# Operand sums formed in temporaries, one tile earlier, and three buffers for a pair's second weight tile

## The chip, the cores and the metric

The kernel runs on one core of a Trainium2 chip. The metric is the device time of one execution in microseconds (us). Five queues work side by side: PE (TensorE, matrix products), DVE (VectorE), ACT (ScalarE), POOL (GpSimd) and SP (which issues the weight loads). Each works through its instructions in a fixed order and waits in place for what an instruction needs.

## The reference

Two transformer blocks over 512 tokens of width 1024, all in fp32. The second block has two layers, each a mixer followed by the MLP that the change is in:

```python
for i in range(DEPTH_2):
    hn = _rmsnorm(h, mix_norm_g[i])
    h = h + (_retention(hn, ...) if i % N_MIXERS == 0 else _chunk_attention(hn, ...))
    h = h + _sqrelu_mlp(_rmsnorm(h, mlp_norm_g[i]), mlp_w1[i], mlp_w2[i])

def _sqrelu_mlp(h, w1, w2):      # w1: 1024 x 4096, w2: 4096 x 1024
    u = jax.nn.relu(h @ w1)
    return (u * u) @ w2
```

## The kernel before

**Layout.** Activations lie transposed, 128 channels by 512 tokens to a tile; `xs[0..7]` is the residual stream. An fp32 product is made of three reduced-precision products: each operand has a high half, which ACT copies (line 130), and a low half, which DVE subtracts (line 114). A weight tile `wr` (128x1024) becomes `wh` and `wl`; activations and weight sums become a `pair` of halves.

**An MLP** (`mlp`) goes through four groups. A group makes eight tiles of hidden units from `w1`, then multiplies them with eight tiles of `w2` and adds the results to `xs`. The first six tiles of group 0 are plain products. Every other tile of `w1` is made in pairs by `Quarters.two`: two weight tiles and the two halves of the tokens are treated as a 2x2 matrix of blocks, with seven block products in place of eight, 12 matmuls each. There is one pair in group 0 and four in each of the other groups, 13 in an MLP.

**What a pair needs.** `Quarters.prepare(k)` makes the four sums of the operand's blocks from `xs[k]` and `xs[k+4]`: two scaled copies by ACT (lines 255 and 256), four DVE operations of 128x256, then the split into halves `q0k` and `q1k`. It is called four times in group 0, and its results serve all 13 pairs. `Quarters.weights` loads the pair's first weight tile into `wr` and its second into `b` (tag `qr`), and POOL makes four sums of their blocks, t1, t2, t4, t3 in this order (`total`, line 283), each split into halves by ACT and DVE. Up to here, `prepare` forms its sums in a tile of the same tag `qr`, which has two buffers, and t1 and t2 have two buffers of a tag `qs` of their own; t3 and t4 take temporaries (`tmp`, a pool of eight buffers of 128x512, that everything uses).

**A pair on PE**: product 1 (weights as loaded), copied by ACT into `u`; product 2 (s1, the halves of t1, with sums 0 of all four k), copied into `v`; the pending last product of the pair before; product 3 (s2), added onto product 1 and copied into `u`; a12; s4, after which DVE forms u + z (line 111) and ends tile j; s3, after which DVE forms x1 (line 111, 128x256). The product with a22 is left pending, and then tile j+1 ends. To end a tile is `square_relu`: DVE line 1088, ACT line 1089 (a square), then the halves of `hid[j]`.

**Order.** PE's order is as the program is written. The other queues are ordered by a scheduler that takes priorities and the free buffers into account, so a change of buffers can move instructions on them.

Of the kernel before, what the change touches and what calls it, by code (L numbers as in the profile page):

```python
# [7 lines left out]
F32 = mybir.dt.float32  # L8
# [6 lines left out]
P = 128  # L15
T = 512
# [46 lines left out]
def kernel(  # L63
# [20 lines left out]
    def pair():  # L84
        return ppool.tile([P, 2, T], F32R, tag="p", name="pair")

    def tmp(dt=F32):
        return tpool.tile([P, T], dt, tag="t", name="tmp")

    def bank(n=T):  # L90
        return psum.tile([P, n], F32, tag="b", name="bank")
# [4 lines left out]
    def f32(ap):  # L96
        return ap.bitcast(F32)
# [5 lines left out]
    def g_(name, i):  # L103
        c = GOFF[name] + i
        return gn[:, c:c + 1]
# [4 lines left out]
    def add(out, a, b):  # L110
        dve.tensor_tensor(out=out, in0=a, in1=b, op=ALU.add)  # L111

    def sub(out, a, b):
        return dve.tensor_tensor(out=out, in0=a, in1=b, op=ALU.subtract)  # L114
# [14 lines left out]
    def copy(out, a):  # L129
        act.activation(out, a, AF.Copy)  # L130

    def split(dst, src, rows=slice(0, P), prompt_=False):

        copy(dst[rows, 0, :], src[rows, :])
        last = sub(dst[rows, 1, :], src[rows, :], f32(dst[rows, 0, :]))
        if prompt_:
            prompt.add(last.ins.name)
# [11 lines left out]
    def weight_tiles(pool=None):  # L149
        raw = wpool.tile([P, 8 * P], F32, tag="wr", name="wr")  # L150
        return [raw] + [(pool or wpool).tile([P, 8 * P], F32R, tag=t, name=t) for t in ("wh", "wl")]

    def load_weights(t, src, c):
        raw, hi, lo = t
        sp.dma_start(raw[:, c], src[:, c])
        with tc.high_priority(offset=HW):
            copy(hi[:, c], raw[:, c])
            prompt.add(sub(lo[:, c], raw[:, c], f32(hi[:, c])).ins.name)

    def weights(src, n=8 * P):  # L160
        t = weight_tiles()
        load_weights(t, src, slice(0, n))
        return t[1:]

    def rows(src, mt, k0=0, nk=8):
        return src[mt * P:(mt + 1) * P, k0 * P:(k0 + nk) * P]
# [67 lines left out]
    def together(parts, ends):  # L234

        for i in range(2 * KT - 2):
            next(parts[i % 2])
            yield
        for part, end in zip(parts, ends):
            drain(part)  # L240
            end()
            yield

    class Quarters:
# [6 lines left out]
        def prepare(self, k, gname):  # L251

            hi, lo = (self.pool.tile([P, 4, T // 2], F32R, name=f"q{e}{k}", tag=f"q{e}{k}") for e in range(2))
            p, q = tmp(), tmp()
            act.activation(p, xs[k], AF.Copy, scale=g_(gname, k))
            act.activation(q, xs[k + 4], AF.Copy, scale=g_(gname, k + 4))
            (b11, b12), (b21, b22) = ([a[:, h] for h in HALVES] for a in (p, q))
            t = self.pool.tile([P, 4, T // 2], F32, name="qr", tag="qr", bufs=2)
            sub(t[:, 0, :], b12, b11)
            sub(t[:, 2, :], b22, b12)  # L260
            add(t[:, 1, :], t[:, 2, :], b11)
            sub(t[:, 3, :], b21, t[:, 1, :])
            copy(hi, t)
            sub(lo, t, f32(hi))
            self.sums.append((hi, lo))

        def operand(self, i, j):
# [5 lines left out]
        def weights(self, src, j, k):  # L273

            one = weight_tiles()
            load_weights(one, rows(src, j), slice(0, 8 * P))
            a = one[0]
            b = self.pool.tile([P, 8 * P], F32, name="qr", tag="qr", bufs=2)
            sp.dma_start(b, rows(src, k))
            a11, a12, a21, a22 = a[:, :T], a[:, T:], b[:, :T], b[:, T:]  # L280

            def total(out, x, y, op):
                nc.gpsimd.tensor_tensor(out=out, in0=x, in1=y, op=op)  # L283

            def parts(src):
                pr = pair()
                split(pr, src, prompt_=True)
                return pr[:, 0, :], pr[:, 1, :]

            with tc.high_priority(offset=HQ):  # L290
                t1, t2 = (self.pool.tile([P, T], F32, name="qs", tag="qs", bufs=2) for _ in range(2))
                t3, t4 = tmp(), tmp()
                total(t1, a21, a22, ALU.add)
                s1 = parts(t1)
                total(t2, t1, a11, ALU.subtract)
                s2 = parts(t2)
                total(t4, a12, t2, ALU.subtract)
                s4 = parts(t4)
                total(t3, a11, a21, ALU.subtract)
                s3 = parts(t3)  # L300
                a22 = parts(a22)
            hi, lo = one[1:]
            return (hi[:, :T], lo[:, :T]), (hi[:, T:], lo[:, T:]), a22, s1, s2, s3, s4
# [48 lines left out]
    def pull(gen, n):  # L352
        for _ in range(n):
            next(gen, None)

    def drain(gen):
        for _ in gen:
            pass
# [225 lines left out]
    for kt in range(KT):  # L584
        t = const.tile([P, T], F32, name=f"x{kt}", tag=f"x{kt}")
# [43 lines left out]
    with tc.tile_pool(name="m1", bufs=1) as m1, tc.tile_pool(name="pt1", bufs=1) as ptp:  # L629
# [142 lines left out]
        for i in (1, 0):  # L772
# [3 lines left out]
            for j in range(2):  # L776
                t = tmp()
# [11 lines left out]
        qs = {}  # L789
# [290 lines left out]
    def mlp(i, now, nxt):  # L1080
        norm, hn = now.norm, now.hn
        qpool = tc.tile_pool(name="qp", bufs=1, reuse_waits="tile")
        quarters = Quarters(hn, qpool.__enter__())
        hid = [pair() for _ in range(8)]

        def square_relu(j, ps):
            t = tmp()
            dve.scalar_tensor_tensor(out=t, in0=ps, scalar=0.0, in1=norm.r, op0=ALU.max, op1=ALU.mult)  # L1088
            act.activation(t, t, AF.Square)  # L1089
            split(hid[j], t)  # L1090

        def group(grp):
            r0 = i * 32 + grp * 8
            if grp == 0:

                two = [(bank(), weights(rows(m_w1, r0 + j))) for j in range(2)]
                yield from together([units(ps, w, K8, hn) for ps, w in two],
                                    [lambda j=j, ps=ps: norm.then(lambda: square_relu(j, ps))
                                     for j, (ps, _) in enumerate(two)])
                for j in range(2, 6):  # L1100
                    w = weights(rows(m_w1, r0 + j))
                    ps = bank()
                    yield from units(ps, w, K8, hn)
                    norm.then(lambda j=j, ps=ps: square_relu(j, ps))
                    if j > 2:
                        quarters.prepare(j - 3, now.gname)
                    yield
                quarters.prepare(3, now.gname)
            for j in range(6 if grp == 0 else 0, 8, 2):
                yield from quarters.two(m_w1, r0 + j, r0 + j + 1, lambda u, j=j: square_relu(j, u),  # L1110
                                        lambda u, j=j: square_relu(j + 1, u))

        for grp in range(4):
            gen = group(grp)
            if grp == 0:
                norm.run(gen, *N_MLP[i])
            drain(gen)
            ends = grp == 3 and nxt is None

            def product(mt):  # L1120
                ws, ps = weights(rows(m_w2, i * KT + mt, grp * 8)), bank()
                return units(ps, ws, K8, hid), lambda: second_end(mt, ps)

            def second_end(mt, ps):
                add(xs[mt], xs[mt], ps)
                if ends:
                    final.square(xs[mt])
                elif grp == 3:
                    nxt.take(mt)


            first = together(*zip(*[product(mt) for mt in range(2)]))
            pull(first, 2)
            drain(quarters.last())
            drain(first)
            if grp == 3:
                qpool.__exit__(None, None, None)
            for mt in range(2, KT - 3 if ends else KT):
                w = weights(rows(m_w2, i * KT + mt, grp * 8))
                ps = bank()  # L1140
                drain(units(ps, w, K8, hid))
                add(xs[mt], xs[mt], ps)
                if ends:
                    final.square(xs[mt])
                elif grp == 3:
                    nxt.take(mt)
            if ends:
                finish(hid, [weights(rows(m_w2, i * KT + mt, grp * 8)) for mt in range(KT - 3, KT)])
# [51 lines left out]
    with tc.tile_pool(name="m2", bufs=1, reuse_waits="tile") as m2:  # L1200
        cs = []
        for i in range(2):
            t = m2.tile([P, T], F32, name=f"rc{i}", tag=f"rc{i}")
# [142 lines left out]
    now, nx = nx, Next("mix1")  # L1346
# [224 lines left out]
```

## Time and profile before

| | |
|---|---|
| median of 3 runs | 2018.83 us (2018.65 to 2020.06) |
| profiled execution | 2017.05 us, span 2015.2 us |
| mean granted clock of PE | 0.991 |
| busy | PE 1952.5 us (97%), DVE 1300.4 (65%), ACT 924.6 (46%), POOL 176.2 (9%) |
| MLP of layer 1, of layer 2 | some 1000 to 1350 us, and 1630 to 2015 us |

The span runs from the first to the last instruction. An engine's idle time matters only where PE waits for it.

### The profile page before, as it was taken

The numbers are of one execution on the slowest core, as the hardware profiler recorded it, in microseconds if no ns is written. First come the engines' busy times: TensorE is split into PE (matmuls) and PEld (weight loads), VectorE is DVE, ScalarE is ACT, GpSimd is POOL, SyncE is SP. The second block draws the span as 40 slices with busy tenths as digits, with TensorE's granted clock in tenths as the row PEclk, the third lists the DMA queues.
The fourth block names the chain that finished last, engine by engine and source line by source line (L and its number), as shares of the span: only waits on it lengthen the run. The fifth ranks groups of instructions, "written<-read, shape, count | busy, mean of one in ns | idle before, by whom it ended". The sixth has DMA issues, their size and how long they took to land.

```text
span 2015.2 us, 26327 instructions
## 1 busy us (share of the span) xinstructions
PE 1952.5 (97%) x10284; PEld 1673.0 (83%) x10284; DVE 1300.4 (65%) x2238; ACT 924.6 (46%) x1571; POOL 176.2 (9%) x125
## 2 busy tenths in 40 slices
PE   9999999999999999999997999999999997999998
PEld 7787888888888888888886889898888886889897
DVE  7878953343478565446656667575698976666565
ACT  5776532232245434233444444353576754344352
POOL 1000000000000000000001224220000001324220
PEclk9999999999999999999998999999999998999999
DMA  5122233333232232323222232322322232233321
GB/s 190 58 75 76 84 94 96 104 94 94 91 115 88 85 95 80 102 74 94 74 94 84 94 105 95 108 82 90 98 88 74 71 111 77 94 109 101 105 74 63
DMA packets 59053, 185.46 MB, mean 92 GB/s; under 512 B 6928, under 2 KB 10400, under 8 KB 58928
## 3 DMA queue, kind: packets, MB, share of 16 engines
q1 hardware_dynamic: 53936, 176.02, 27.5%
q10 hardware_dynamic: 4688, 7.40, 1.2%
q8 instruction: 80, 1.31, 0.3%
q14 instruction: 45, 0.37, 0.1%
q0 software_dynamic: 304, 0.36, 0.1%
HBM read 181.56 MB, written 2.20 MB: 91 GB/s over the span
## 4 chain that ended last, share of the span: by engine, by line
issue 57%; PE 30%; DVE 6%; ACT 3%; POOL 2%; DMA 2%; SPq 0%; POOLq 0%; ACTq 0%; DVEq 0%
PE bank L169 7%; PE bank L171 7%; PE bank L170 7%; PE bank L310 6%; DVE wl L114 2%; DMA qr<-in_m_w_dram 1%; DVE pair L114 1%; POOL tmp L283 1%; ACT pair L130 1%; DVE tmp L111 1%; PE bank L526 1%; POOL qs L283 1%; ACT wh L130 1%; DVE tmp L500 0%; DVE tmp L491 0%
## 5 line engine op out<-in xcount | busy, mean ns | idle before, releaser
L169 PE MATMUL bank<-pair,wh 128*128 128x512 f32 (+1 forms) x2134 | 816.4, 383 | 0.2 <-ACT pair L130 0.2
L171 PE MATMUL bank<-pair,wh 128*128 128x512 f32 (+1 forms) x2134 | 807.6, 378 | 0.5 <-DVE pair L114 0.3
L170 PE MATMUL bank<-pair,wl 128*128 128x512 f32 (+1 forms) x2134 | 806.4, 378 | 0.0
L130 ACT ACTIVATE wh<-wr 128x1024 fp32r<-128x1024 f32 (+5 forms) x329 | 324.1, 989 | 653.2 <-PE bank L171 407.7
L114 DVE TENSOR_TENSOR wl<-wr,wh 128x1024 fp32r<-128x1024 f32 (+5 forms) x329 | 383.4, 1168 | 157.1 <-ACT wh L130 155.9
L171 PEld LDWEIGHTS bank<-pair,wh 128*128 128x128 f32 x2134 | 401.4, 188 | 77.0 <-DVE pair L114 1.7
L169 PEld LDWEIGHTS bank<-pair,wh 128*128 128x128 f32 x2134 | 401.9, 188 | 70.9 <-ACT pair L130 0.8
L170 PEld LDWEIGHTS bank<-pair,wl 128*128 128x128 f32 x2134 | 402.0, 188 | 70.4 <-DVE wl L114 0.5
L114 DVE TENSOR_TENSOR pair<-tmp,pair 128x512 fp32r<-128x512 f32 (+1 forms) x208 | 171.2, 830 | 63.7 <-ACT pair L130 60.7
L130 ACT ACTIVATE pair<-tmp 128x512 fp32r<-128x512 f32 (+1 forms) x240 | 149.8, 628 | 130.7 <-POOL tmp L283 54.8
L310 PE MATMUL bank<-q,pair 128*128 128x256 f32 x1248 | 166.4, 287 | 38.8 <-ACT pair L130 26.6
L310 PEld LDWEIGHTS bank<-q,pair 128*128 128x128 f32 x1248 | 157.0, 192 | 44.2 <-ACT pair L130 27.1
L111 DVE TENSOR_TENSOR x<-x,bank 128x512 f32<-128x512 f32 (+1 forms) x99 | 66.0, 669 | 170.0 <-PE bank L171 170.0
L283 POOL TENSOR_TENSOR qs<-qr 128x512 f32<-128x512 f32 x26 | 40.9, 1573 | 1478.0 <-DMA qr<-in_m_w_dram 1478.0
L108 DVE TENSOR_TENSOR tmp<-bank,rb 128x512 f32<-128x512 f32 (+1 forms) x76 | 50.2, 666 | 103.9 <-PE bank L171 101.3
L310 PE MATMUL bank<-pair,wh 128*128 128x256 f32 x416 | 83.0, 283 | 0.0
L169 PE MATMUL bank<-wh,pair 128*128 128x512 f32 x200 | 79.3, 396 | 0.6 <-ACT tmp L130 0.6
L171 PE MATMUL bank<-wl,pair 128*128 128x512 f32 x200 | 78.0, 390 | 0.0
L170 PE MATMUL bank<-wh,pair 128*128 128x512 f32 x200 | 77.9, 390 | 0.0
L494 ACT ACTIVATE tmp<-tmp,small 128x512 f32<-128x512 f32 (+1 forms) x96 | 53.4, 556 | 34.1 <-DVE small L491 32.9
L310 PEld LDWEIGHTS bank<-pair,wh 128*128 128x128 f32 x416 | 67.8, 190 | 0.8 <-ACT tmp L130 0.2
L1089 ACT ACTIVATE tmp<-tmp 128x512 f32<-128x512 f32 x64 | 40.1, 627 | 61.1 <-DVE tmp L1088 61.1
(182 smaller groups left out, 2010.2 us busy)
## 6 DMA issues: line engine op xcount, KB each, us to landing
wr<-in_m_w_dram SPq DMA_DIRECT2D x102, 512.0 KB, 3.7
wr<-in_r_qkg_dram SPq DMA_DIRECT2D x32, 512.0 KB, 3.5
qr<-in_m_w_dram SPq DMA_DIRECT2D x26, 512.0 KB, 3.7
wr<-in_w_gate_dram SPq DMA_DIRECT2D x20, 512.0 KB, 3.5
wr<-in_w_up_dram SPq DMA_DIRECT2D x20, 512.0 KB, 3.5
wr<-in_w_down_dram SPq DMA_DIRECT2D x16, 512.0 KB, 3.4
wr<-in_r_v_dram SPq DMA_DIRECT2D x16, 512.0 KB, 3.5
wr<-in_r_out_dram SPq DMA_DIRECT2D x16, 512.0 KB, 3.7
```

What stands on the lines that cost most here:

```text
L108: dve.tensor_tensor(out=out, in0=a, in1=b, op=ALU.mult)
L111: dve.tensor_tensor(out=out, in0=a, in1=b, op=ALU.add)
L114: return dve.tensor_tensor(out=out, in0=a, in1=b, op=ALU.subtract)
L130: act.activation(out, a, AF.Copy)
L169: pe.matmul(out, lhsT=ah, rhs=bh, start=start, stop=False)
L170: pe.matmul(out, lhsT=al, rhs=bh, start=False, stop=False)
L171: pe.matmul(out, lhsT=ah, rhs=bl, start=False, stop=stop)
L283: nc.gpsimd.tensor_tensor(out=out, in0=x, in1=y, op=op)
L310: pe.matmul(out, lhsT=x[:, c], rhs=y, start=start and k + i == 0, stop=k == 3 and i == 2, skip_group_check=True)
L494: act.activation(s[:, :n], s[:, :n], AF.Exp, bias=self.mx[:, col], scale=-1.0, accum_out=self.sm[:, col])
L526: pe.matmul(o, lhsT=a, rhs=b, start=j == 0 and a is v, stop=j == NT - 1 and a is v)
L1089: act.activation(t, t, AF.Square)
```

## The change

`prepare` forms its four sums in two temporaries `s` and `t` of 128x512, with two sums each, and splits each of them on its own; it is called for k = 0 to 3 after the plain tiles 2 to 5, where before it came for k = 0 to 2 after tiles 3 to 5 and for k = 3 behind them. `b` alone uses the tag `qr` now, with three buffers. t1 and t2 become temporaries as well, and the tag `qs` is gone.

```diff
--- before.py
+++ after.py
@@ -255,13 +255,14 @@
             act.activation(p, xs[k], AF.Copy, scale=g_(gname, k))
             act.activation(q, xs[k + 4], AF.Copy, scale=g_(gname, k + 4))
             (b11, b12), (b21, b22) = ([a[:, h] for h in HALVES] for a in (p, q))
-            t = self.pool.tile([P, 4, T // 2], F32, name="qr", tag="qr", bufs=2)
-            sub(t[:, 0, :], b12, b11)
-            sub(t[:, 2, :], b22, b12)
-            add(t[:, 1, :], t[:, 2, :], b11)
-            sub(t[:, 3, :], b21, t[:, 1, :])
-            copy(hi, t)
-            sub(lo, t, f32(hi))
+            s, t = (tmp().rearrange("p (e t) -> p e t", e=2) for _ in range(2))
+            sub(s[:, 0, :], b12, b11)
+            sub(t[:, 0, :], b22, b12)
+            add(s[:, 1, :], t[:, 0, :], b11)
+            sub(t[:, 1, :], b21, s[:, 1, :])
+            for e, a in ((slice(0, 2), s), (slice(2, 4), t)):
+                copy(hi[:, e, :], a)
+                sub(lo[:, e, :], a, f32(hi[:, e, :]))
             self.sums.append((hi, lo))
 
         def operand(self, i, j):
@@ -275,7 +276,7 @@
             one = weight_tiles()
             load_weights(one, rows(src, j), slice(0, 8 * P))
             a = one[0]
-            b = self.pool.tile([P, 8 * P], F32, name="qr", tag="qr", bufs=2)
+            b = self.pool.tile([P, 8 * P], F32, name="qr", tag="qr", bufs=3)
             sp.dma_start(b, rows(src, k))
             a11, a12, a21, a22 = a[:, :T], a[:, T:], b[:, :T], b[:, T:]
 
@@ -288,8 +289,7 @@
                 return pr[:, 0, :], pr[:, 1, :]
 
             with tc.high_priority(offset=HQ):
-                t1, t2 = (self.pool.tile([P, T], F32, name="qs", tag="qs", bufs=2) for _ in range(2))
-                t3, t4 = tmp(), tmp()
+                t1, t2, t3, t4 = (tmp() for _ in range(4))
                 total(t1, a21, a22, ALU.add)
                 s1 = parts(t1)
                 total(t2, t1, a11, ALU.subtract)
@@ -1102,10 +1102,8 @@
                     ps = bank()
                     yield from units(ps, w, K8, hn)
                     norm.then(lambda j=j, ps=ps: square_relu(j, ps))
-                    if j > 2:
-                        quarters.prepare(j - 3, now.gname)
+                    quarters.prepare(j - 2, now.gname)
                     yield
-                quarters.prepare(3, now.gname)
             for j in range(6 if grp == 0 else 0, 8, 2):
                 yield from quarters.two(m_w1, r0 + j, r0 + j + 1, lambda u, j=j: square_relu(j, u),
                                         lambda u, j=j: square_relu(j + 1, u))
```

**DVE between the first and the second pair of group 1.** The rows are of the first MLP, before. `tmp_9389` and `bank_9387` belong to the pair that ends, `pair_9494`, `_9498` and `_9501` are the low halves of s4, s3 and a22 of the pair that begins, `pair_9620` and `pair_9624` those of s1 and s2 of the third pair, `pair_8664` and `pair_8665` are hidden tiles.

```order
L111 TENSOR_TENSOR tmp_9389<-tmp_9389,bank_9388 128x512
L111 TENSOR_TENSOR bank_9387<-tmp_9390,bank_9387 128x256
L1088 SCALAR_TENSOR_TENSOR tmp_9455<-tmp_9389,rb_8768 128x512
L114 TENSOR_TENSOR pair_9494<-tmp_9484,pair_9494 128x512
L114 TENSOR_TENSOR pair_9498<-tmp_9483,pair_9498 128x512
L114 TENSOR_TENSOR pair_9501<-qr_9479,pair_9501 128x512
L114 TENSOR_TENSOR pair_9620<-qs_9615,pair_9620 128x512
L114 TENSOR_TENSOR pair_8664<-tmp_9455,pair_8664 128x512
L1088 SCALAR_TENSOR_TENSOR tmp_9546<-bank_9387,rb_8768 128x512
L114 TENSOR_TENSOR pair_9624<-qs_9616,pair_9624 128x512
L114 TENSOR_TENSOR pair_8665<-tmp_9546,pair_8665 128x512
```

The same place after the change; `pair_9498` and `pair_9502` are s1 and s2 of the pair that begins, `pair_9506`, `_9510` and `_9513` its s4, s3 and a22:

```order
L111 TENSOR_TENSOR tmp_9401<-tmp_9401,bank_9400 128x512
L111 TENSOR_TENSOR bank_9399<-tmp_9402,bank_9399 128x256
L1088 SCALAR_TENSOR_TENSOR tmp_9467<-tmp_9401,rb_8768 128x512
L114 TENSOR_TENSOR pair_9498<-tmp_9493,pair_9498 128x512
L114 TENSOR_TENSOR pair_9502<-tmp_9494,pair_9502 128x512
L114 TENSOR_TENSOR pair_9506<-tmp_9496,pair_9506 128x512
L114 TENSOR_TENSOR pair_9510<-tmp_9495,pair_9510 128x512
L114 TENSOR_TENSOR pair_9513<-qr_9491,pair_9513 128x512
L114 TENSOR_TENSOR pair_8664<-tmp_9467,pair_8664 128x512
L1088 SCALAR_TENSOR_TENSOR tmp_9558<-bank_9399,rb_8768 128x512
L114 TENSOR_TENSOR pair_8665<-tmp_9558,pair_8665 128x512
```

The low halves of s1 and s2 stood a pair ahead of their use, and now stand behind the end of the pair before (the `bank_9399` row, line 111) and ahead of everything else of their own pair.

**POOL, the sums of the second to fourth pair of group 1.** Before (a `DVE` in the brackets is a wait for a DVE instruction, a `DMAHW` one for a load, and `qs_9615`, `qs_9616` are t1 and t2 of the third pair):

```order
L283 TENSOR_TENSOR qs_9615<-qr_9613 128x512 [waits DMAHW4_49,DVE_49,Pool_49]
L283 TENSOR_TENSOR tmp_9484<-wr_9473,qs_9482 128x512
L283 TENSOR_TENSOR tmp_9483<-wr_9473,qr_9479 128x512
L283 TENSOR_TENSOR qs_9616<-qs_9615,wr_9607 128x512 [waits DMAHW5_49,DVE_49,Pool_49]
L283 TENSOR_TENSOR qs_9749<-qr_9747 128x512 [waits DMAHW0_49,DVE_49,Pool_49]
L283 TENSOR_TENSOR tmp_9618<-wr_9607,qs_9616 128x512
L283 TENSOR_TENSOR tmp_9617<-wr_9607,qr_9613 128x512
```

After the change, t1, t2, t4, t3 of the third pair and the first two of the fourth:

```order
L284 TENSOR_TENSOR tmp_9627<-qr_9625 128x512 [waits DMAHW7_49,DVE_49,Pool_49]
L284 TENSOR_TENSOR tmp_9628<-tmp_9627,wr_9619 128x512 [waits DMAHW6_49,DVE_49,Pool_49]
L284 TENSOR_TENSOR tmp_9630<-wr_9619,tmp_9628 128x512 [waits DVE_49,Pool_49]
L284 TENSOR_TENSOR tmp_9629<-wr_9619,qr_9625 128x512 [waits DMAHW5_49,DVE_49]
L284 TENSOR_TENSOR tmp_9761<-qr_9759 128x512 [waits DMAHW5_49,DVE_49,Pool_49]
L284 TENSOR_TENSOR tmp_9762<-tmp_9761,wr_9753 128x512 [waits DMAHW7_49,DVE_49,Pool_49]
```

Every sum waits for DVE now, since every one takes a temporary that some earlier low half must have been read from; before, in groups 1 to 3, only t1 and t2 did so, for the `qs` buffer of the pair before.

**DVE ahead of the first pair**, before: `q12` and `q13` are low halves of the sums for k = 2 and 3, `pair_8979` that of s1.

```order
L111 TENSOR_TENSOR qr_8959<-qr_8959,tmp_8955 128x256
L114 TENSOR_TENSOR wl_9092<-wr_9090,wh_9091 128x1024
L114 TENSOR_TENSOR q12_8941<-qr_8946,q02_8940 128x1024
L114 TENSOR_TENSOR qr_8959<-tmp_8956,qr_8959 128x256
L114 TENSOR_TENSOR q13_8954<-qr_8959,q03_8953 128x1024
L114 TENSOR_TENSOR pair_8979<-qs_8974,pair_8979 128x512
L114 TENSOR_TENSOR pair_8983<-qs_8975,pair_8983 128x512
L114 TENSOR_TENSOR pair_8987<-tmp_8977,pair_8987 128x512
```

And after the change (`tmp_8968` and `tmp_8969` are `s` and `t` of k = 3, `pair_8991` is the low half of s1, `pair_8995` that of s2):

```order
L111 TENSOR_TENSOR tmp_8968<-tmp_8969,tmp_8964 128x256
L114 TENSOR_TENSOR pair_8669<-tmp_8957,pair_8669 128x512
L114 TENSOR_TENSOR pair_8991<-tmp_8986,pair_8991 128x512
L114 TENSOR_TENSOR tmp_8969<-tmp_8965,tmp_8968 128x256
L114 TENSOR_TENSOR pair_8995<-tmp_8987,pair_8995 128x512
L114 TENSOR_TENSOR pair_8999<-tmp_8989,pair_8999 128x512
L114 TENSOR_TENSOR pair_9003<-tmp_8988,pair_9003 128x512
L114 TENSOR_TENSOR pair_9006<-qr_8984,pair_9006 128x512
L114 TENSOR_TENSOR q13_8963<-tmp_8968,q03_8962 128x512
L114 TENSOR_TENSOR q13_8963<-tmp_8969,q03_8962 128x512
```

The halves of the last operand sums, which stood ahead of the weights' halves, stand behind all of them.

**SP, the weight loads between retention and the first MLP**, one piece of the difference; `qr` is the load of `b`:

```order
 L155 DMA wr<-in_r_qkg_dram 128x1024 x4
-L155 DMA wr<-in_r_out_dram 128x1024 x8
-L155 DMA wr<-in_m_w_dram 128x1024 x11
-L279 DMA qr<-in_m_w_dram 128x1024 x2
+L155 DMA wr<-in_r_out_dram 128x1024 x2
+L280 DMA qr<-in_m_w_dram 128x1024 x3
+L155 DMA wr<-in_r_out_dram 128x1024 x6
+L155 DMA wr<-in_m_w_dram 128x1024 x12
```

The first three loads of `b` move ahead of the MLP's own loads, in among those of retention's output weights. The second MLP has the same move into the loads of `a_out`.

## Rows read from the trace of the kernel before

**Rows 1.** The page, part 1: busy us, share, instructions.
```profile
PE 1952.5 (97%) x10284; PEld 1673.0 (83%) x10284; DVE 1300.4 (65%) x2238; ACT 924.6 (46%) x1571; POOL 176.2 (9%) x125
```

**Rows 2.** Waits of PE over the span: waited for, us in total, times, longest.
```profile
PE bank L310 <- ACT pair L130: 26.6, 2, 13.5
PE bank L310 <- ACT tmp L130: 10.3, 12, 1.7
```

**Rows 3.** Timeline, first pair of the first MLP: start, us, engine, line, operation.
```profile
1073.26 0.69 DVE L1088 SCALAR_TENSOR_TENSOR tmp<-bank,rb 128x512 f32<-128x512 f32 x1 [0.19 <-PE bank L171]
...
1079.94 1.22 DVE L114 TENSOR_TENSOR q<-qr,q 128x1024 fp32r<-128x1024 f32 x1
...
1081.23 3.01 SPq L279 DMA_DIRECT2D qr<-in_m_w_dram  x2
...
1082.62 1.23 DVE L114 TENSOR_TENSOR q<-qr,q 128x1024 fp32r<-128x1024 f32 x1 [1.12 <-ACT q L130]
1085.82 1.25 POOL L283 TENSOR_TENSOR qs<-qr 128x512 f32<-128x512 f32 x1 [1045.66 <-DMA qr<-in_m_w_dram]
1087.11 0.63 ACT L130 ACTIVATE pair<-qs 128x512 fp32r<-128x512 f32 x1 [4.52 <-POOL qs L283]
...
1087.79 0.58 PE L310 MATMUL bank<-q,pair 128*128 128x256 f32 x1 [13.14 <-ACT pair L130]
...
1089.02 1.22 PE L310 MATMUL bank<-q,pair 128*128 128x256 f32 x4 [0.65 <-DVE pair L114]
```

**Rows 4.** Windows around that restart; before DMA share and GB/s stands PEclk.
```profile
1080.00:1086.00 6.00, 0.00 (x0) 0.00 (x0) 2.72 (x4) 1.06 (x1) 0.18 (x1) 0.50 0.63 203
...
1092.00:1094.00 2.00, 2.00 (x16) 1.85 (x16) 1.85 (x3) 1.64 (x4) 1.50 (x1) 0.98 0.47 119
```

**Rows 5.** PE's timeline, group 1: the first products of two successive pairs.
```profile
1151.33 0.28 PE L310 MATMUL bank<-pair,wh 128*128 128x256 f32 x1
...
1161.68 0.28 PE L310 MATMUL bank<-pair,wh 128*128 128x256 f32 x1
```

**Rows 6.** DVE's timeline in the pairs of group 1.
```profile
1162.09 0.67 DVE L111 TENSOR_TENSOR tmp<-tmp,bank 128x512 f32<-128x512 f32 x1
1162.69 0.42 DVE L111 TENSOR_TENSOR bank<-tmp,bank 128x256 f32<-128x256 f32 x1
...
1163.80 2.38 DVE L114 TENSOR_TENSOR pair<-tmp,pair 128x512 fp32r<-128x512 f32 x2
1166.11 0.68 DVE L114 TENSOR_TENSOR pair<-qr,pair 128x512 fp32r<-128x512 f32 x1
...
1182.11 1.22 DVE L114 TENSOR_TENSOR wl<-wr,wh 128x1024 fp32r<-128x1024 f32 x1 [0.26 <-ACT wh L130]
```

**Rows 7.** POOL's timeline in the same stretch.
```profile
1161.05 2.28 POOL L283 TENSOR_TENSOR tmp<-wr,qr 128x512 f32<-128x512 f32 x1
1163.29 1.75 POOL L283 TENSOR_TENSOR qs<-qs,wr 128x512 f32<-128x512 f32 x1
```

**Rows 8.** ACT's timeline in the same stretch.
```profile
1168.63 0.63 ACT L1089 ACTIVATE tmp<-tmp 128x512 f32<-128x512 f32 x1 [1.49 <-DVE tmp L1088]
1169.17 0.36 ACT L130 ACTIVATE tmp<-bank 128x256 f32<-128x256 f32 x1
...
1169.95 1.05 ACT L130 ACTIVATE wh<-wr 128x1024 fp32r<-128x1024 f32 x1
```

**Rows 9.** Groups of DVE by shape, 1190 to 1225: busy, mean ns, idle before.
```profile
L114 DVE TENSOR_TENSOR pair<-tmp,pair 128x512 fp32r<-128x512 f32 x2 | 3.1, 1552 | 0.3 <-ACT pair L130 0.2
```

**Rows 10.** Windows ahead of the second MLP; last DMA share and GB/s.
```profile
1622.00:1631.00 9.00, 9.00 (x41) 7.46 (x40) 7.34 (x13) 5.23 (x9) 0.00 (x0) 1.00 0.19 66
1631.00:1634.00 3.00, 3.00 (x15) 2.46 (x15) 2.90 (x6) 2.58 (x5) 0.00 (x0) 1.00 0.57 175
```

**Rows 11.** Timeline at the second MLP's second weight tile.
```profile
1638.77 1.23 DVE L114 TENSOR_TENSOR wl<-wr,wh 128x1024 fp32r<-128x1024 f32 x1
...
1640.33 0.39 PE L170 MATMUL bank<-pair,wl 128*128 128x512 f32 x1
```

## The prediction

> **What bounds the kernel now.** I read the page's busy times first: PE is busy for 97% of the span and no other engine for more than 65% [rows 1], so a change counts only where it lengthens or shortens a wait of PE. The list of PE's waits comes next. Two lines of it belong to the pairs (line 310): one long wait ahead of the first pair of each MLP, 26.6 us in two, and 10.3 us in twelve short waits for an ACT copy into a temporary, two in each of the six groups 1 to 3 [rows 2]. These 36.9 us are what the change can touch.
>
> The timeline of the first pair tells what the long wait is for. PE has run dry 13.14 us before 1087.79. The low halves for k = 2 are DVE's 1079.94 row; they are the last reader of a `qr` buffer, so SP issues the load of `b` at 1081.23, POOL starts t1 at 1085.82, ACT's copy is at 1087.11, PE gets one matmul at 1087.79 and the rest from 1089.02 [rows 3]. Behind this chain a second one is hidden: the low halves for k = 3, which the same product needs, are made from 1082.62 for 1.23 us [rows 3]. So without the late load the product could have ended its wait only at 1083.9 even then. The windows show PE's granted clock at 0.50, the 1.2 GHz level, in 1080 to 1086, after some microseconds without a matmul, and at 0.98 in 1092 to 1094 [rows 4]. So what resumes before 1092 may run at half rate.
>
> For the steady pairs, one product 1 stands at 1151.33 and the next at 1161.68: 10.35 us for seven products where PE hardly waits, 1.48 each [rows 5].
>
> **A. The first pair: -5.5 us in both MLPs together.** The load of `b` leaves the path: it has buffers of its own and is issued long before. What is late next is DVE, by its new order. The plain tile 5 ends where it did, and DVE's line 1088 for it starts at 1073.26 [rows 3]. Behind it stand, start to start: itself 0.6, a `wl` 1.14 (the row of 1.22 [rows 6], less the overlap of some 0.08 between rows that follow each other at once), three operations of 128x256 at 0.42 (the nearest row of this size [rows 6]), a hidden tile's low half 0.6 (0.68 alone [rows 6]); that is 1076.85. Then s1's low half, one more operation of 0.42, the low halves of s2, s4, s3 and a22, and only then k = 3. POOL works on the sums meanwhile (1.25 us alone, 1.75 to 2.28 beside DVE [rows 3, 7]), so I cost these five as contended, 1.45 each (below): 1076.85 + 5 x 1.45 + 0.42 + 0.6 = 1085.1 for the first half of k = 3, which product 2 needs. Before, the three matmuls that need k = 3 came some 1.8 us after 1089.02, eight matmuls later at half rate (0.21 from the row of four [rows 3]), at 1090.8. Gain 5.7 us. From it goes the clock: if PE stays at half rate until 1092 as before, 6.9 us of work are worth 3.45, where before 1.2 us were worth 0.6, a loss of 2.85. Net 2.8 for each MLP, 5.5 for two. Ends: 0, if PE's scattered matmuls come later still or the clock stays low for longer; -15, if the clock never falls and the five low halves run half alone.
>
> **B. The steady pairs: +27 us.** Formerly a pair's s1 and s2 were made up to a pair ahead, from buffers that nobody else used. Now POOL's t1 can start only when an earlier low half has been read, so each POOL sum is released by a DVE subtraction of the running pair, and POOL's four sums run under the four subtractions that follow. At the same time s1 and s2 of the beginning pair stand in DVE's queue behind x1, which needs the last product of the pair before. I walk one cycle of DVE and ACT from the start of one s1 low half to the next; a DVE row of 0.68 counts 0.61, start to start.
>
> s1 0.61. s2 must wait for its high half, which ACT copies behind the square of tile j (0.63 [rows 8], a copy about as much): s2 starts at 1.33 and ends its turn at 1.94. Then s4, s3, a22 and hidden tile j, all under POOL. Price of one: 0.61 if alone; 1.15 by the two that took 2.38 us beside POOL's 1163.29 row, which covers only their first part [rows 6, 7]; 1.55 in the w2 tiles, where POOL ran throughout [rows 9]. I take 1.36, between the last two, since POOL's four sums at 1.75 are longer than the four subtractions: 1.94 + 5.44 = 7.38. Line 1088 for tile k is behind them, 8.06. ACT squares it (0.63) and only then copies product 3 into `u` (0.36 [rows 8]): 9.0. PE's s3 product overwrites what this copy reads, and PE would be ready at 7.9 (six products of 1.48 after product 1, which starts 1.0 ahead of s1: x1 at 0.34 and line 1088 at 0.61). Stall 1.1. ACT goes on with k's high half and the `wh` of 1.05 [rows 8] until 10.5; DVE's `wl` (1.22 [rows 6]) to 11.7; u + z 0.60 and x1 0.34 (0.67 and 0.42 [rows 6]), line 1088 0.61: the next s1 starts at 13.25, and is ready at 13.9 where PE, after its stall, has wanted it since 11.9. Stall 1.9. A cycle is 13.25 against 10.35: 2.9 us more. A group has two such cycles, and a first s1 that is 0.35 late: 2 x 2.9 + 0.35 = 6.15. Six groups: 36.9. The 10.3 us of short waits go [rows 2], since they are of the same kind and are contained in the walk: +26.6, say +27.
>
> Ends: with 0.61 each the cycle is 10.25, nothing but the 0.35 stays, 2.1 - 10.3 = -8. With 1.55 each it is 14.0, 7.65 a group, 45.9 - 10.3 = +36.
>
> A rule speaks to this price. The Trainium skill (page "SBUF — State Buffer", section "Who interferes with whom") says that DVE with two SBUF inputs and GpSimd share a port pair as an exclusive lock. If that meant a whole POOL sum ahead of each subtraction, the row of 1.55 [rows 9] would have been 0.68 + 1.25 = 1.93, so the trace shows less than strict turns; that case is the third rival.
>
> **C. The loads: +1 us.** Three loads of `b` (128x1024 fp32, 0.52 MB each) move in among those of `a_out`, ahead of the second MLP. In 1622 to 1631 66 GB/s flowed, and 175 just behind [rows 10]: room for 109 GB/s x 9 us = 0.98 MB of their 1.57; the rest holds the MLP's first weights up by 0.59 MB / 175 GB/s = 3.4 us if none of it went earlier. The second tile's `wl` ends at 1640.00 and PE uses it at 1640.33 [rows 11], so 0.3 us are free. Ends 0 and 3 for each MLP; I take 1 for both, because earlier stretches have room too. Splitting `prepare`'s halves in two pieces adds eight ACT and eight DVE rows in an MLP's one-time preparation; they are in walk A.
>
> **Sum.** 2017.05 - 5.5 + 27 + 1 = 2039.5 for the profiled execution. The runs' median is 1.78 above that execution, so 2041.3 in terms of the median: 2041.
>
> **Rivals.** (1) Contention half as wide: POOL covers two of the four subtractions. The cycle is 11.75, 1.4 over; 6 x (2.8 + 0.35) - 10.3 = +9, and the time 2023. For it: POOL's sums wait for loads before, and any such shift would move them. Against: their waits are now for DVE itself.
> (2) Other side, faster: POOL's sums fall into DVE's free time (DVE is idle for 35% of the span [rows 1]), the cycle stays under 10.35, B is -8, and the first pair gains in full with the clock up, 2 x 6.2: 2018.83 - 8 - 12.4 = 1998. It decides at the price of 0.63 for a subtraction in the cycle, where the cycle is 10.35. Against: every row of a subtraction beside POOL is well above.
> (3) Strict turns: 1.93 per subtraction, cycle 15.5, 5.2 over; 6 x (10.4 + 0.35) - 10.3 = +54, and the time 2068.
> (4) The change does not do what it says for the first pair: PE waits for k = 3 as long as it waited for the load, A is 0: 2047. For it: k = 3 now stands last on DVE.
>
> **How the numbers follow.** Chances: forecast 0.63, rival (1) 0.12, (2) 0.10, (3) 0.07, (4) 0.08. The likeliest case's own range is 2030 to 2050 (B's price of 1.2 to 1.55, A's ends in part). The range reaches down to (1) and up past (4), 2018 to 2056; it leaves out (2), (3) and some of each tail. A change of under 0.2%, 4 us, is about what a measurement of this kernel can't tell from none: half of (1) and some tail of (2) lie there, 0.08. Faster is (2) for the rest and a little of B's low tail, 0.11. Slower is 0.81.
>
> **What would show it.** In the changed profile: PE's one long wait ahead of a first pair is replaced by two or three of 3 to 4 us, the last of them for a DVE low half of `q`, and the next products end some 3 us earlier than before relative to tile 5. In groups 1 to 3 PE waits for a DVE `pair` (line 114) about 1.9 us and for an ACT `tmp` about 1.1 us in two pairs of each group. POOL's rows (line 284) lie under DVE rows of 1.2 to 1.6 us. PE's clock stays at 1.00 in these pairs. The prediction is wrong if DVE's subtractions between s2 and line 1088 take under 1 us each, if POOL's sums come ahead of the running pair, or if PE's short stalls pull the clock to 0.5, which would add to the time beyond the range.

## The result and the profile after

| | before | changed |
|---|---|---|
| median | 2018.91 us (4 runs) | 2039.65 us (2038.91 to 2040.86, 4 runs) |
| ratio | | 1.0102, 95% interval 1.0085 to 1.012 |
| profiled execution, span | 2017.05, 2015.2 us | 2039.02, 2037.0 us |
| mean granted clock | 0.991 | 0.992 |

The change makes the kernel 20.7 us slower. The forecast was 2041 us, with 0.81 for slower.

Where the time went can be read from PE's timelines: the stretch from the start of the first to the start of the last matmul of the pairs (line 310), for the lone pair of group 0 and for the four pairs of each other group. The two MLPs are set one after the other.

| us | before | changed | difference |
|---|---|---|---|
| first pair | 27.35, 27.73 | 23.97, 24.05 | -7.1 |
| groups 1 to 3 | 43.65, 44.44, 43.40, 44.21, 44.44, 43.29 | 48.75, 48.73, 48.74, 48.74, 48.73, 48.73 | +29.0 |
| span | 2015.2 | 2037.0 | +21.8 |

The two differences make 21.9, so what happened elsewhere comes to little in all. PE's list of waits says the same (waited for, us in total, times, longest), where before it had [rows 2]:

```profile
PE bank L310 <- DVE pair L114: 27.0, 20, 3.2
PE bank L310 <- ACT tmp L130: 12.7, 12, 1.1
PE bank L310 <- ACT pair L130: 7.1, 2, 3.9
...
PE bank L310 <- DVE q L114: 3.8, 2, 1.9
```

The two waits of 13 us are gone, and 20 waits for DVE's low halves have come, with twelve for ACT's copies, as many as before and longer on the mean (12.7 us in all for 10.3), though the longest is shorter.

**A steady pair.** PE's timeline of the changed kernel, two successive pairs of group 1 (start, us, operation, and in brackets the idle time before it and its releaser):

```profile
1150.07 4.63 PE L310 MATMUL bank<-q,pair 128*128 128x256 f32 x35 [0.17 <-DVE pair L114]
...
1158.61 1.69 PE L310 MATMUL bank<-q,pair 128*128 128x256 f32 x12 [1.04 <-ACT tmp L130]
...
1163.47 4.62 PE L310 MATMUL bank<-q,pair 128*128 128x256 f32 x35 [1.63 <-DVE pair L114]
```

From one product 2 to the next it is 13.40 us, where before two successive pairs stood 10.35 us apart if no wait fell between them [rows 5]. There are two stalls in it, one of 1.04 for ACT's copy into `u` ahead of s3, and one of 1.63 for the low half of s1. DVE's timeline over the same pair:

```profile
1148.39 0.43 DVE L111 TENSOR_TENSOR bank<-tmp,bank 128x256 f32<-128x256 f32 x1
1148.72 0.69 DVE L1088 SCALAR_TENSOR_TENSOR tmp<-tmp,rb 128x512 f32<-128x512 f32 x1
1149.33 0.69 DVE L114 TENSOR_TENSOR pair<-tmp,pair 128x512 fp32r<-128x512 f32 x1
1150.63 3.00 DVE L114 TENSOR_TENSOR pair<-tmp,pair 128x512 fp32r<-128x512 f32 x3 [0.62 <-ACT pair L130]
1153.55 1.77 DVE L114 TENSOR_TENSOR pair<-qr,pair 128x512 fp32r<-128x512 f32 x1
1155.25 1.78 DVE L114 TENSOR_TENSOR pair<-tmp,pair 128x512 fp32r<-128x512 f32 x1
1156.95 0.68 DVE L1088 SCALAR_TENSOR_TENSOR tmp<-bank,rb 128x512 f32<-128x512 f32 x1
...
1162.13 0.68 DVE L1088 SCALAR_TENSOR_TENSOR tmp<-tmp,rb 128x512 f32<-128x512 f32 x1
...
1180.97 0.68 DVE L114 TENSOR_TENSOR pair<-tmp,pair 128x512 fp32r<-128x512 f32 x1
```

Here the queue can be read as the order has it: x1 (1148.39, 128x256) must wait for the pair before, line 1088 for tile j follows, then s1 (1149.33), a wait of 0.62 for ACT, s2, s4, s3 (three in 3.00 us), a22 1.77, the hidden tile j 1.78, and only at 1156.95 line 1088 for tile k, on which ACT's copy into `u` waits. From 1148.72 to 1162.13 it is 13.41 us, DVE's cycle. The last row is the same subtraction two cycles on, when POOL's sum had ended at 1180.50: it takes 0.68 us, where the one at 1155.25 takes 1.78. POOL's timeline:

```profile
1151.45 1.62 POOL L284 TENSOR_TENSOR tmp<-qr 128x512 f32<-128x512 f32 x1 [20.39 <-DVE pair L114]
1153.15 1.62 POOL L284 TENSOR_TENSOR tmp<-tmp,wr 128x512 f32<-128x512 f32 x1
1154.85 1.63 POOL L284 TENSOR_TENSOR tmp<-wr,tmp 128x512 f32<-128x512 f32 x1
1157.10 1.28 POOL L284 TENSOR_TENSOR tmp<-wr,qr 128x512 f32<-128x512 f32 x1 [0.62 <-DVE pair L114]
```

The first and the fourth sum begin as one of DVE's subtractions gives up a temporary; the second and third follow the sum before them at once. The first three run from 1151.45 to 1156.48, just while DVE is at s3, a22 and j. A window over such a pair has the clock in the third column from the end: it stays up through these stalls.

```profile
1149.00:1163.00 14.00, 11.63 (x92) 10.87 (x90) 11.64 (x14) 6.82 (x14) 6.14 (x4) 1.00 0.15 46
```

**The first pair.** PE's timeline has three waits in place of the long one [rows 3]:

```profile
1078.00 0.56 PE L310 MATMUL bank<-q,pair 128*128 128x256 f32 x1 [3.11 <-ACT pair L130]
1081.79 2.50 PE L310 MATMUL bank<-q,pair 128*128 128x256 f32 x10 [3.23 <-DVE pair L114]
1086.21 3.14 PE L310 MATMUL bank<-q,pair 128*128 128x256 f32 x13 [1.92 <-DVE q L114]
...
1091.71 1.59 PE L310 MATMUL bank<-pair 128*128 128x256 f32 x12
```

DVE's timeline, with the low halves for k = 2, line 1088 of tile 5, the hidden tile and s1, the low halves of s2, s4, s3, then a22, and last the two of k = 3:

```profile
1072.64 2.39 DVE L114 TENSOR_TENSOR q<-tmp,q 128x512 fp32r<-128x512 f32 x2
1074.95 0.68 DVE L1088 SCALAR_TENSOR_TENSOR tmp<-bank,rb 128x512 f32<-128x512 f32 x1
...
1079.37 2.37 DVE L114 TENSOR_TENSOR pair<-tmp,pair 128x512 fp32r<-128x512 f32 x2
...
1081.99 1.88 DVE L114 TENSOR_TENSOR pair<-tmp,pair 128x512 fp32r<-128x512 f32 x3
1083.80 1.75 DVE L114 TENSOR_TENSOR pair<-qr,pair 128x512 fp32r<-128x512 f32 x1
1085.47 1.28 DVE L114 TENSOR_TENSOR q<-tmp,q 128x512 fp32r<-128x512 f32 x2
```

PE goes on at 1086.21 with the last matmul of product 2, after the first of the two low halves for k = 3, as the order had it. It is the only one of the twelve that needs this half: one and ten have run by then, and the row of 13 is that one and the twelve of product 3. The windows show the clock at the 1.2 GHz level from 1078 on, and up again between 1090 and 1092:

```profile
1078.00:1080.00 2.00, 0.56 (x1) 0.26 (x1) 1.97 (x5) 0.52 (x1) 0.78 (x2) 0.51 0.71 219
...
1090.00:1092.00 2.00, 2.00 (x12) 2.00 (x12) 0.00 (x0) 0.09 (x1) 0.00 (x0) 0.57 0.00 0
```

### The profile page after: what moved, and what is told of

Same layout as the page of the kernel before. It is cut to its first block, busy times and chain, and to the rows that moved or that the text cites. A ratio compares the mean times of both kernels' runs of the same rounds, so it can differ in the third digit from the quotient of the medians.

```text
span 2037.0 us, 26315 instructions
## 1 busy us (share of the span) xinstructions
PE 1962.6 (96%) x10284; PEld 1677.1 (82%) x10284; DVE 1325.7 (65%) x2246; ACT 920.9 (45%) x1579; POOL 181.3 (9%) x125
## 4 chain that ended last, share of the span: by engine, by line
PE 74%; DVE 14%; ACT 6%; issue 5%; POOL 0%; DMA 0%; POOLq 0%; ACTq 0%; DVEq 0%
PE bank L169 22%; PE bank L171 22%; PE bank L170 22%; PE bank L310 5%; DVE pair L114 4%; DVE wl L114 3%; ACT pair L130 2%; ACT wh L130 1%; DVE tmp L111 1%; DVE tmp L1088 1%; PE bank L526 1%; ACT tmp L494 1%; PE bank L507 1%; DVE pt L114 1%; DVE tmp L491 1%
## 5 line engine op out<-in xcount | busy, mean ns | idle before, releaser
L114 DVE TENSOR_TENSOR pair<-tmp,pair 128x512 fp32r<-128x512 f32 (+1 forms) x260 | 220.3, 862 | 71.9 <-ACT pair L130 70.2
L310 PE MATMUL bank<-q,pair 128*128 128x256 f32 x1248 | 174.1, 291 | 50.6 <-DVE pair L114 27.0
L130 ACT ACTIVATE pair<-tmp 128x512 fp32r<-128x512 f32 (+1 forms) x292 | 177.8, 624 | 96.2 <-DVE tmp L1306 26.0
L284 POOL TENSOR_TENSOR tmp<-qr 128x512 f32<-128x512 f32 x26 | 43.2, 1662 | 1538.5 <-DVE tmp L114 1032.8
L111 DVE TENSOR_TENSOR tmp<-tmp 128x512 f32<-128x512 f32 (+1 forms) x98 | 60.4, 617 | 14.7 <-ACT tmp L379 13.8
```

What stands on the lines that cost most here:

```text
L310: pe.matmul(out, lhsT=x[:, c], rhs=y, start=start and k + i == 0, stop=k == 3 and i == 2, skip_group_check=True)
```

## The experiments

Each was run beside the kernel before on the same chip, whose medians were 2018.6, 2017.6 and 2018.5 us in the three sets; ratios are to these. A statement's line number can differ by one between the kernels: 309 or 311 stands for 310, and 1089 for 1088.

**e1: the change without its last part.** t1 and t2 keep `qs`, and `b` has two buffers, for which the room suffices.

```diff
-            b = self.pool.tile([P, 8 * P], F32, name="qr", tag="qr", bufs=3)
+            b = self.pool.tile([P, 8 * P], F32, name="qr", tag="qr", bufs=2)
...
-                t1, t2, t3, t4 = (tmp() for _ in range(4))
+                t1, t2 = (self.pool.tile([P, T], F32, name="qs", tag="qs", bufs=2) for _ in range(2))
+                t3, t4 = tmp(), tmp()
```

Expected: 

> The change without its last part: prepare's sums in temporaries and one tile earlier, b with two buffers of its own, but t1 and t2 keep the two buffers of qs. My theory (the loss is that t1 and t2 took temporaries): the steady pairs are as before, with PE's short waits back at some 10 us in twelve and no DVE waits of 1.6 us; the first pair keeps its gain of 3 us or more in each MLP. 2012 us (2008 to 2016). Rival (the loss comes from prepare's temporaries, or from the loads that moved): the time stays at 2035 or above.

Measured 2007.64 us (2006.28 to 2008.79), ratio 0.9947 (0.993 to 0.9963). Faster than the kernel before, and just under the range expected. PE's waits:

```profile
PE bank L311 <- ACT tmp L130: 9.9, 12, 1.7
PE bank L311 <- ACT pair L130: 7.0, 2, 3.9
...
PE bank L311 <- DVE q L114: 3.9, 2, 1.9
PE bank L311 <- DVE pair L114: 2.3, 2, 1.2
```

The short waits are back where they were [rows 2] and the six groups take 262.95 us in all, against 263.43 before. The two first pairs take 21.43 and 21.61 us, 12.0 less than before, and 5.0 less than in the changed kernel. What has shrunk is the wait for the low half of s1, 1.2 us at most where it was 3.2. POOL's t1 and t2 run as soon as the loads are there, far ahead of the first pair, and only the sums in temporaries are left for the end of tile 5:

```profile
983.20 1.29 POOL L284 TENSOR_TENSOR qs<-qr 128x512 f32<-128x512 f32 x1 [941.39 <-DMA qr<-in_m_w_dram]
1058.85 1.30 POOL L284 TENSOR_TENSOR qs<-qs,wr 128x512 f32<-128x512 f32 x1 [74.36 <-DMA wr<-in_m_w_dram]
1075.10 1.59 POOL L284 TENSOR_TENSOR tmp<-wr,qs 128x512 f32<-128x512 f32 x1 [14.95 <-DVE tmp L114]
```

So the loss isn't in prepare's temporaries nor in the loads. (The first pair begins 2.4 us later in this execution than before, and 1.6 us later in e2, whose work up to there is that of the kernel before. Some 1.5 us of either arise between 168 and 174 us, where the mean granted clock is 0.72 in both and 1.00 before; in e1 the rest is there by 30 us. Both lie far ahead of what the edits touch.)

**e2: the last part alone**, in the kernel before:

```diff
-                t1, t2 = (self.pool.tile([P, T], F32, name="qs", tag="qs", bufs=2) for _ in range(2))
-                t3, t4 = tmp(), tmp()
+                t1, t2, t3, t4 = (tmp() for _ in range(4))
```

Expected: 

> The last part alone: the kernel before with t1 and t2 in temporaries. My theory: the cycles of 13.4 us in the steady pairs are there in full, the long wait of 13 us ahead of each first pair stays, 2018.9 + 27 = 2046 us (2040 to 2050). Rival: the pairs are slow only together with the other parts, 2019 us.

Measured 2048.74 us (2047.52 to 2050.44), ratio 1.015 (1.0135 to 1.0165), 30.2 us slower. The waits of both kinds stand side by side, the long one of the first pair and the many of the steady pairs:

```profile
PE bank L309 <- ACT pair L130: 26.9, 2, 13.5
PE bank L309 <- DVE pair L114: 21.8, 20, 1.6
PE bank L309 <- ACT tmp L130: 12.6, 12, 1.1
```

The six groups take 292.35 us, as in the changed kernel (292.42). With e1 this splits the change: temporaries for t1 and t2 cost some 29 us, and the rest of the change is a gain.

**e3: the sums on DVE.** In the changed kernel:

```diff
-                nc.gpsimd.tensor_tensor(out=out, in0=x, in1=y, op=op)
+                dve.tensor_tensor(out=out, in0=x, in1=y, op=op)
```

Expected: 

> The changed kernel with the four sums of a pair's weights made by DVE in place of POOL, so that POOL never runs beside DVE, and DVE has four operations of 0.6 us more in each pair. My theory (DVE's subtractions take 1.7 in place of 0.6 us while POOL runs, some 3.3 us a pair): that falls away and 2.4 us come in, so a cycle goes from 13.4 to 12.6 us, and the time to about 2030 us (2024 to 2036). Rival (contention costs nothing, the order of the queue does): a cycle is 2.4 us longer, 15.8, and the time 2065 or more.

Measured 2023.4 us (2021.8 to 2025.45), ratio 1.0025 (1.0015 to 1.0036), just under the range expected and 16 us less than the changed kernel, although DVE has 104 operations more. DVE's timeline, one cycle from line 1088 to line 1088:

```profile
1148.45 0.69 DVE L1088 SCALAR_TENSOR_TENSOR tmp<-tmp,rb 128x512 f32<-128x512 f32 x1
...
1150.43 0.69 DVE L114 TENSOR_TENSOR pair<-tmp,pair 128x512 fp32r<-128x512 f32 x1
...
1152.85 1.89 DVE L114 TENSOR_TENSOR pair<-tmp,pair 128x512 fp32r<-128x512 f32 x3
1154.65 0.68 DVE L114 TENSOR_TENSOR pair<-qr,pair 128x512 fp32r<-128x512 f32 x1
1155.26 0.68 DVE L1088 SCALAR_TENSOR_TENSOR tmp<-bank,rb 128x512 f32<-128x512 f32 x1
...
1160.32 0.69 DVE L1088 SCALAR_TENSOR_TENSOR tmp<-tmp,rb 128x512 f32<-128x512 f32 x1
```

Every subtraction takes its 0.61, start to start, and the cycle is 11.87 in place of 13.41 us. I had expected 12.6: the wait of 0.6 us ahead of s2 is gone too, since DVE has sums to make in that time. The cycle became 1.54 us shorter although four sums came in (4 x 0.61, of which 0.6 filled that wait: 1.84), so contention of POOL and DVE had cost 3.4 us a cycle. That is three subtractions at 1.70 in place of 0.61, 3.3. The rival, that only the order counts, is out. Without contention and without the sums on DVE the cycle would be 11.87 - 1.84 = 10.0 us, under the 10.35 of before [rows 5]; this is worked out and was not run. Of the 16 us the six groups make 10.9 (281.47 us in all) and the two first pairs 5.2 (21.16 and 21.69 us). A group is 1.9 us shorter and not 2 x 1.54, since its first s1 comes later, behind two sums on DVE: PE waits 0.96 and 0.34 us there, where it waited 0.17.

**e5: two buffers for `b`** in the changed kernel (`bufs=3` to `bufs=2`).

Expected: 

> The changed kernel with two buffers for b in place of three. My theory (POOL's sums in the steady pairs wait for temporaries, not for loads): nothing changes in the pairs' groups, 48.7 us each, and the time stays that of the changed kernel, 2039.7 us (2037 to 2042). Rival (the third buffer carries a gain that the rest hides, or a loss by its early loads): 2043 or above, or 2036 or below, with a wait for a load ahead of POOL's sums in the first case.

Measured 2040.38 us (2038.72 to 2044.12), ratio 1.0115 (1.01 to 1.013): as the changed kernel, within what can be told. PE's list has the same leading row, and the groups 48.72 to 48.74 us each:

```profile
PE bank L310 <- DVE pair L114: 27.1, 20, 3.3
```

The third buffer does nothing. What moved the load off the path of the first pair is that `prepare` gave up the tag.

**e8: prepare as late as before**, otherwise e1:

```diff
-                    quarters.prepare(j - 2, now.gname)
+                    if j > 2:
+                        quarters.prepare(j - 3, now.gname)
                     yield
+                quarters.prepare(3, now.gname)
```

Expected: 

> e1 with prepare called where it was before, for k = 0 to 2 after tiles 3 to 5 and for k = 3 behind them; its sums are still in temporaries and b is loaded early. My theory (with the load gone from the path, DVE's work behind tile 5 sets the first pair): one more prepare, some 3 us of DVE, stands behind tile 5, and each first pair is 3 us longer than in e1: 2013.6 us (2010 to 2017). Rival (the load alone made the wait): as e1, 2007.6 us.

Measured 2012.31 us (2011.59 to 2012.78), ratio 0.9973 (0.9962 to 0.9983). The first pairs take 25.06 and 24.80 us, 3.4 more each than in e1. DVE's timeline from line 1088 of tile 5 to the last halves for k = 3:

```profile
1074.82 0.68 DVE L1089 SCALAR_TENSOR_TENSOR tmp<-bank,rb 128x512 f32<-128x512 f32 x1
...
1087.65 1.47 DVE L114 TENSOR_TENSOR q<-tmp,q 128x512 fp32r<-128x512 f32 x2
```

The last low halves begin 12.8 us behind line 1088 of tile 5 (here 1089), where in e1 they began 8.4 behind it (1085.54 against 1077.16). So both edits count: the load off the path, and the earlier call.

**e7: prepare one tile earlier still**, in e1, after the first two tiles together and tiles 2 to 4:

```diff
+                quarters.prepare(0, now.gname)
                 for j in range(2, 6):
...
-                    quarters.prepare(j - 2, now.gname)
+                    if j < 5:
+                        quarters.prepare(j - 1, now.gname)
```

Expected: 

> e1 with prepare called one more tile earlier, after the first two tiles and tiles 2, 3 and 4. My theory (the first pair waits since DVE makes the halves for k = 3 and the weights' halves after tile 5): k = 3 is ready by tile 5, the wait ahead of the first pair falls to 3 us or less, the clock does not fall, and each MLP loses some 10 us more: 1992 us (1986 to 2002). Rival (the work is only moved, and delays tiles 2 to 5 by as much): 2010 us or more, with new waits of PE in the plain tiles.

Measured 1999.74 us (1997.89 to 2001.26), ratio 0.9906 (0.9891 to 0.9921), inside the range expected, but not for the whole of its reason: the plain tiles have no new waits and PE waits no more for `q`, yet a wait for ACT's copies of the weight sums is left ahead of product 2:

```profile
PE bank L311 <- ACT pair L130: 8.2, 2, 4.8
```

These copies stand behind the end of tile 5 in ACT's queue, 3.4 us in the first MLP and 4.8 in the second where 3 or less was expected, and the clock falls there too (0.50 in 1080 to 1084). The first pairs take 18.19 and 18.63 us. My theory had named only half of what is late.

**e9: the first pair's weight sums ahead of tile 5**, in e7:

```diff
                     ps = bank()
+                    if j == 5:
+                        ahead = quarters.weights(m_w1, r0 + 6, r0 + 7)
                     yield from units(ps, w, K8, hn)
```

and the first pair takes `ahead` in place of a call of its own.

Expected: 

> e7 with the weight sums of the first pair issued ahead of plain tile 5, so that ACT and DVE make their halves before they end tile 5. My theory (what is left of the first pair's wait in e7 is ACT's copies of these sums behind the end of tile 5): the wait of 3.4 and 4.8 us falls under 1, the clock stays up, and the time is 1988 us (1983 to 1995). Rival (ACT and DVE are full there, and what is moved ahead delays tile 5 or the first weight tile of the pair by as much): 1998 us or more, with a new wait of PE in plain tile 5 or in product 1.

Measured 1995.44 us (1992.96 to 1997.55), ratio 0.9887 (0.987 to 0.9903), at the upper end of the range expected. The ratio's interval overlaps that of e7; the gain over e7 is read from the first pairs, which take 14.42 and 16.39 us, 6.0 less in two. The wait for ACT's copies is gone, and another has come, for DVE's low half of k = 3, which the weights' halves have passed in the queue; 2.66 us in the first MLP:

```profile
1082.47 2.02 PE L311 MATMUL bank<-q,pair 128*128 128x256 f32 x13 [2.66 <-DVE q L114]
```

In spite of this wait the clock stays up in the first MLP, which it did in none of the kernels above (the window holds the wait); in the second, behind a wait of 3.00 us, it is 0.77 in 1670 to 1674 and 0.61 in 1674 to 1676:

```profile
1080.00:1084.00 4.00, 1.53 (x11) 1.39 (x12) 4.00 (x8) 1.92 (x5) 0.00 (x0) 1.00 0.41 91
```

**e10: prepare in the scheduler's high priority**, in e9:

```diff
-                        quarters.prepare(j - 1, now.gname)
+                        with tc.high_priority(offset=HQ):
+                            quarters.prepare(j - 1, now.gname)
```

Expected: 

> e9 with prepare in the scheduler's high priority, so that the halves for k = 3 stand among the first two of the weights' halves and no longer behind them all and behind the end of tile 5. My theory (what is left of the first pair's wait in e9, 5.7 us in two, is DVE's place for k = 3): this wait falls under 1 us in two, and the time is 1990 us (1986 to 1994). Rival (DVE is full there, so that the pair waits as long for the next thing in its queue): as e9, 1994 us or more, with waits of the same sum for a low half of the weights.

Measured 1990.18 us (1988.82 to 1992.89), ratio 0.9863 (0.9846 to 0.9879), as expected: no wait for `q` is left in the list. Its first line is that of the steady pairs, with two more waits, of 1.2 and 0.5 us, in the first pairs; the second MLP's first pair also waits 1.2 us for an ACT copy and 0.9 us for a low half.

```profile
PE bank L311 <- ACT tmp L130: 10.6, 14, 1.7
...
PE bank L311 <- ACT pair L130: 1.2, 1, 1.2
```

The first pairs take 12.88 and 14.93 us, against 27.35 and 27.73 before. This is the fastest version, 28 us under the kernel before and 49 under the changed one.

## Why the prediction was right

**A, the first pair: -5.5 forecast, -7.1 measured.** The mechanism was right in its parts. The load left the path, DVE's queue took its place, k = 3 came last, and the 1.2 GHz level took part of the gain. Two sizes were wrong, and they partly cancel. The kernel before, from the matmul after s1's low half to a row that can be set beside 1091.71 in the changed one:

```profile
1089.02 4.35 PE L310 MATMUL bank<-q,pair 128*128 128x256 f32 x23 [0.65 <-DVE pair L114]
...
1094.84 1.60 PE L310 MATMUL bank<-pair 128*128 128x256 f32 x12
```

The walk took three matmuls to need the low halves for k = 3, and had the first half ready at 1085.1. Only one needs it; it ran at 1091.32 before and at 1086.21 after, 5.1 us earlier (5.3 from the pair's start) where the walk gave 5.7. The walk's start was wrong as well: line 1088 of tile 5 is not at 1073.26 but at 1074.95, behind the low halves for k = 2, which took 2.39 us while POOL was at t1; the three low halves after 1081.99 gave part of it back, with 1.88 us together where I had costed each as contended. The other size is the clock's: from that matmul to the last row above there are 25, and they took 3.5 us before and 5.5 after, a loss of 2.0 where I had 2.85. In the second MLP the two are 4.9 from the pair's start and 1.2. So the gain was put too high and the loss to the clock still more so, and the term came out 1.6 too small in two.

**B, the steady pairs: +27 forecast, +29.0 measured.** The cycle was walked as 13.25 us and is 13.41; stalls of 1.1 and 1.9 us were expected where 1.04 and 1.63 stand. The four subtractions under POOL were priced at 1.36 each, 5.44 in all. What they did is otherwise: s4 ran free at some 0.61, and the three others took 1.70 start to start (1153.55, 1155.25, 1156.95), 5.7 in all. So the mean was nearly right, which is in part luck, and the price of a contended one was low: the rows beside POOL that I had were partly covered [rows 6, 9]. The first s1 of a group holds PE up by 0.34 us: product 2's second matmul starts at 1150.07, 0.46 behind the first one at 1149.61, where PE's pace is 0.12; the walk had 0.35. A group lost 4.8 us and the walk gave 4.4; the cycle's 0.16, twice, is most of the difference, and I have not followed the rest.

**C, the loads: +1 forecast, +0.3 measured.** The first pair of the first MLP begins 0.24 us later. From the last pair of the first MLP to the first pair of the second it is 314.68 us before (1358.89 to 1673.57) and 314.74 after (1370.42 to 1685.16). The room was larger than the estimate had it: in 1633 to 1643, where the three loads went out among the last ones of `a_out`, 224 GB/s flowed, above the 175 that I had taken as the most. The MLP's own loads begin at 1642.42 where they began at 1630.82, 11.6 later, of which the first MLP had lost 11.5.

**The sum.** The errors of A and B are of opposite sign, 1.6 and 2.0, so the sum is nearer to the result than its terms are. That nearness is luck.

**The rivals.** Half contention (2023 us) and the case of contention-free sums (1998) fall with the 1.70 of the rows. That the first pair gains nothing (2047) falls with its 23.97 us. Strict turns (2068) expected 1.93 for a subtraction; the row is 1.70, and only three of four were caught. By the Trainium skill (page "SBUF — State Buffer", section "Who interferes with whom") the two engines lock each other out. The trace agrees in direction, and e3 shows that the loss is gone once POOL rests. But one sum and one subtraction together take 1.70 us where they take 1.29 and 0.61 alone, 1.90. That rules out the price of 1.93 and not turns as such: the ends of the rows do alternate, DVE's 0.55 us behind POOL's (1153.07 and 1153.63, 1154.77 and 1155.32, 1156.48 and 1157.03) and POOL's 1.15 behind DVE's.

**What stays open.** e1 and e2 show that the loss comes with t1 and t2 in temporaries, and e3 that POOL beside DVE is what makes the cycle long. Whether more temporaries than eight would let POOL work ahead again was not run.

## What to carry to other kernels

A buffer of its own for work that runs ahead is worth more than its size: t1 and t2 took 4 KB of each partition, and to put them into a shared pool made POOL's sums wait for subtractions in DVE's queue and put the two engines side by side on the pairs of groups 1 to 3. Ask of each freed buffer who has to give it up, at what place in its queue, and what will then run at the same time. And when a long wait is taken away, walk the next queue in its order up to the end: here it was the load, then DVE's k = 3, then ACT's copies, then k = 3 again, and each step behind the load was worth some 3 to 8 us.

## What the runs showed of the hardware

Where DVE's subtractions and POOL's sums both have work waiting, they go in step: DVE begins one at 1151.84 (the third of the row of three), 1153.55 and 1155.25, POOL at 1151.45, 1153.15 and 1154.85, one of each in every 1.70 us, though DVE's alone takes 0.61 and POOL's 1.29. Operations of DVE that read PSUM, such as line 1088 at 1156.95 with 0.68 (it reads a `bank`, and POOL's fourth sum ran from 1157.10), show no such stretch.

PE's clock fell to its lower level in the first pair of every kernel but the last two, each time in or behind an idle stretch of 2.5 us or more. In e9 it stayed at 1.00 behind one of 2.66 us in the first MLP and fell for a short time behind one of 3.00 in the second; in e10, and in the changed kernel's steady pairs with stalls of 1.63 us, it stayed up. The length of one wait does not tell what it will do. In group 1 of e9 it fell behind a stall of 1.72 us (0.59 in 1170 to 1172 and 0.55 in 1172 to 1174; that group took 45.67 us, and 44.13 in e10, where it stayed at 1.00 behind one of 1.71). At 169 us it fell in e1 behind a wait of 2.25 us, while the kernel before had waited 2.28 there and kept 1.00.
